# Other layouts for the moving operands and outputs of the products in a one-core encoder layer

## The chip, the cores and the metric

The kernel runs on one core of one Trainium2 chip. The metric is the time of the whole program on the device in microseconds, taken from the host's runs; a profiled execution gives the trace. Engines: PE (TensorE) multiplies, with its weight loads recorded apart as PEld; ACT (ScalarE), DVE (VectorE) and POOL (GpSimd) work on whole tiles; SP issues most DMAs. SBUF is the buffer that operands lie in, PSUM the accumulators that PE writes.

## What is computed

One layer of a streaming encoder on 320 token columns (256 of a prompt, 64 of a running stream), model width 2048. Cut to what the change touches:

```python
proj = xn @ w_in[l]                       # q, k, v, u, vs and two gates, 2048 columns each gate
a = stick_breaking(q, k, v)               # 8 heads x 128
bb = spatial_gate(u, vs, w_s, b_s)        # 8 groups x 128
gates = sigmoid(g + b_gate[l])
merged = g_a * (a @ w_branch_a[l]) + g_b * (bb @ w_branch_b[l])
h = x + merged @ w_out[l]
hn = rmsnorm(h, norm_ffn[l])
gu = hn @ w_gate_up[l]                    # D_FF = 5632
h = h + (silu(gu[..., :D_FF]) * gu[..., D_FF:]) @ w_down[l]
```

## The kernel before

Activations lie with features on the 128 partitions and the 320 token columns along them. Each float32 product is made from three products in the type float32r: weights and activations are each split into a rounded half (hi) and a rest (lo), and `product` adds hi times hi, hi times lo and lo times hi into one PSUM tile. One call of `product` is three matmuls of 128x128 weights with 320 moving columns: line 79 moves x[0] (hi) under the hi weights, line 80 moves x[1] (lo) under the same weights, line 81 moves x[0] under the lo weights.

`block` makes one output block of 128 features. It runs over its input blocks in groups of at most 8 (`HALF`): `weights` loads a group from HBM through SP (line 68), ACT makes its hi half (line 71), DVE its lo half (line 72), and then come the calls of `product`. Three PSUM tiles "acc" and four pairs of weight halves rotate.

`split` makes hi (ACT, line 113) and lo (DVE, line 114) of an activation, in two separate tiles "B" of 320 words a partition. Three families of activations go through it: the 8 heads' outputs `aT`, the 8 groups' outputs `bT`, and the hidden activations `act` of the feed-forward part. `gained` (lines 119 and 120) does the same for the inputs "A" with a gain per feature, and the merge makes its own pairs (mh, ml).

In order of time: the projections of q, k, v with attention woven in; v and u of the spatial gate; the merge, 16 times (two gate blocks from `w_in`, one block from `w_a` with `aT`, one from `w_b` with `bT`); 16 blocks of `w_out`; then three slices of the feed-forward part (16, 16 and 12 of its 44 blocks), each with its gate and up blocks from `w_gu` and 16 blocks of `w_down` that add to h. The last norm and the output follow.

A scheduler puts each engine's instructions in order by its own estimate; SP's order in the first stage is written by hand, and `tick`/`at` hang small pieces (attention, norms) between the groups of weights.

Of the kernel before, what the change touches and what calls it, by code (L numbers as in the profile page):

```python
# [9 lines left out]
F32R = mybir.dt.float32r  # L10
# [3 lines left out]
P = 128  # L14
TP = 256
TS = 64
T = TP + TS
D = 2048
KD = D // P
H = 8  # L20
# [3 lines left out]
SLICES = ((0, 16), (16, 16), (32, 12))  # L24
# [7 lines left out]
def stream_step(ctx: ExitStack, tc: tile.TileContext, xT, w_in, w_a, w_b, w_out, w_gu, w_down,  # L32
                gains, ws_t, bs, ck_t, cv, y_t, k_t, v_t, sv_t):
    nc = tc.nc
# [4 lines left out]
    big = pool("big")  # L39
# [3 lines left out]
    def acc():  # L43
        return psum.tile([P, 512], F32, tag="acc", bufs=3, name="acc")
# [15 lines left out]
    def tick():  # L60
        state["tick"] += 1
        for fn, a in later.pop(state["tick"], ()):
            fn(*a)


    def weights(src, n, view=lambda t: t):
        raw = wraw.tile([P, HALF * P], F32, tag="raw", name="raw")
        nc.sync.dma_start(out=view(raw[:, : n * P]), in_=src)
        wh = wsplit.tile([P, HALF * P], F32R, tag="wh", name="wh")
        wl = wsplit.tile([P, HALF * P], F32R, tag="wl", name="wl")  # L70
        nc.scalar.copy(out=wh[:, : n * P], in_=raw[:, : n * P])  # L71
        nc.vector.tensor_tensor(out=wl[:, : n * P], in0=raw[:, : n * P],  # L72
                                in1=wh[:, : n * P].bitcast(F32), op=ALU.subtract)
        return wh, wl

    def product(ps, w, j, x, first, last):
        wh, wl = w
        a, b = wh[:, j * P : (j + 1) * P], wl[:, j * P : (j + 1) * P]
        nc.tensor.matmul(ps[:, :T], a, x[0], start=first, stop=False)  # L79
        nc.tensor.matmul(ps[:, :T], a, x[1], start=False, stop=False)  # L80
        nc.tensor.matmul(ps[:, :T], b, x[0], start=False, stop=last)  # L81

    def block(src, act):

        ps = acc()
        nk = len(act)
        for k0 in range(0, nk, HALF):
            n = min(HALF, nk - k0)
            w = weights(src[:, k0 * P : (k0 + n) * P], n)
            for j in range(n):  # L90
                product(ps, w, j, act[k0 + j], k0 + j == 0, k0 + j == nk - 1)
            tick()
        return ps[:, :T]

    def slot(tag):
        return big.tile([P, T], F32R, tag=tag, bufs=32, name=tag)
# [11 lines left out]
            out.append(t[:, i % 2 * T : (i % 2 + 1) * T])  # L108
        return out, both

    def split(tag, src):
        hi, lo = slot(tag), slot(tag)
        nc.scalar.copy(out=hi, in_=src)
        nc.vector.tensor_tensor(out=lo, in0=src, in1=hi.bitcast(F32), op=ALU.subtract)
        return hi, lo
# [69 lines left out]
    xs = []  # L185
    first = [aux() for _ in range(3)]
# [12 lines left out]
    with tc.manual_schedule(engines={mybir.EngineType.SP}):  # L199
        load_x(*steps[0])  # L200
        for i, (c, n) in enumerate(steps):
            w = weights(w_qkv[0, :, :, c * P : (c + n) * P], 3 * n,
                        lambda t: t.rearrange("p (b k) -> p b k", b=3))
            if i + 1 < len(steps):
                load_x(*steps[i + 1])
            x = xp[c // 2]
            for m in range(c, c + n):
                xs.append(gained("A", x[:, m % 2 * T : (m % 2 + 1) * T], g_mix[:, m : m + 1]))
            for b in range(3):
                for j in range(n):  # L210
                    product(first[b], w, n * b + j, xs[c + j], c + j == 0, c + j == KD - 1)
            if c == 1:
                nc.scalar.activation(out=sqx, in_=x, func=AF.Square)
            elif c > 1:
                s = pair("xx")
                if c % 4:
                    nc.gpsimd.tensor_tensor(out=s, in0=x, in1=x, op=ALU.mult)
                else:
                    nc.scalar.activation(out=s, in_=x, func=AF.Square)
                (nc.gpsimd if c % 4 else nc.vector).tensor_tensor(out=sqx, in0=sqx, in1=s, op=ALU.add)  # L220
# [119 lines left out]
    def att_out(p, j):  # L340
        s = attn[p]
        (w0, w1), (vn, own_v), cvt = s["zm"], s["vn"][j], s["cv"]
        po = aux1()

        lo = 256 - 64 * j
        for i in range(3):
            v = cvt[:, i, j, :] if i < 2 else own_v
            nc.tensor.matmul(po[:, lo : lo + P], v, w1[:, 256 + i * P : 256 + (i + 1) * P],  # L348
                             start=i == 0, stop=i == 2)
        nc.tensor.matmul(po[:, 0:256], vn[:, 0, :], w0[:, j * 256 : (j + 1) * 256], start=True, stop=False)  # L350
        nc.tensor.matmul(po[:, 128:256], vn[:, 1, :], w1[:, j * P : (j + 1) * P], start=False, stop=True)
        aT[2 * p + j] = split("B", po[:, 0:T])

    aT: dict[int, tuple] = {}
    got = {}
# [35 lines left out]
    for g in range(H):  # L391
        ps = block(w_in[4 * H + g], xs)
        t = t320("ev")
# [18 lines left out]
    def sgu_mix(g):  # L412
        vn, own_v = vnat.pop(g)
        pg = aux()
        nc.tensor.matmul(pg[:, 256:384], own_v, wst[:, g, :], start=True, stop=True)
        nc.tensor.matmul(pg[:, 0:128], vn[:, 0, :], wst[:, g, :], start=True, stop=True)
        nc.tensor.matmul(pg[:, 128:256], vn[:, 1, :], wst[:, g, :], start=True, stop=True)
        b = t320("bb")
        for lo, n in ((0, 128), (128, 128), (256, 64)):
            nc.vector.tensor_tensor(out=b[:, lo : lo + n], in0=pg[:, lo : lo + n], in1=bsb[:, g, 0:n], op=ALU.add)  # L420
        nc.vector.tensor_tensor(out=b, in0=b, in1=us[g], op=ALU.mult)
        bT[g] = split("B", b)

    base = state["tick"]
    at(base + 1, sgu_norm)
# [3 lines left out]
    for g in range(H):  # L429
        ps = block(w_in[3 * H + g], xs)  # L430
        t = t320("ev")
# [6 lines left out]
    for m in range(KD):  # L438
        gate = []
        for i in range(2):  # L440
            ps = block(w_in[5 * H + i * KD + m], xs)
            t = t320("ev")
            nc.vector.tensor_tensor(out=t, in0=ps, in1=got["rx"], op=ALU.mult)
            gt = t320(f"gate{i}", 1)
            nc.scalar.activation(out=gt, in_=t, func=AF.Sigmoid, bias=b_gate[:, i * KD + m : i * KD + m + 1])
            gate.append(gt)
        if m == 0:
            att_ctx.close()
            mpool = mctx.enter_context(tc.tile_pool(name="merged", bufs=1))
        ps = block(w_a[m], [aT[h] for h in range(H)])  # L450
        t = t320("mg", 1)
        nc.vector.tensor_tensor(out=t, in0=ps, in1=gate[0], op=ALU.mult)
        ps = block(w_b[m], [bT[g] for g in range(H)])
        nc.vector.tensor_tensor(out=gate[1], in0=ps, in1=gate[1], op=ALU.mult)
        nc.vector.tensor_tensor(out=t, in0=t, in1=gate[1], op=ALU.add)
        hi = mpool.tile([P, T], F32R, tag="C", bufs=32, name="mh")
        lo = mpool.tile([P, T], F32R, tag="C", bufs=32, name="ml")
        nc.scalar.copy(out=hi, in_=t)
        nc.vector.tensor_tensor(out=lo, in0=t, in1=hi.bitcast(F32), op=ALU.subtract)
        merged.append((hi, lo))  # L460
# [4 lines left out]
    for m in range(KD):  # L465
        x = t320("xr")
        nc.gpsimd.dma_start(out=x, in_=xT[:, m, :])
        ps = block(w_out[m], merged)
# [8 lines left out]
    last = const.tile([P, T], F32, name="last")  # L477
    for s0, n in SLICES:
        act = []
        pend = []  # L480

        def finish(pg, pu):
            t = t320("ev")
            nc.vector.tensor_tensor(out=t, in0=pg, in1=got["rh"], op=ALU.mult)  # L484
            nc.scalar.activation(out=t, in_=t, func=AF.Silu)
            u = t320("bb")
            nc.vector.tensor_tensor(out=u, in0=pu, in1=got["rh"], op=ALU.mult)  # L487
            nc.vector.tensor_tensor(out=u, in0=u, in1=t, op=ALU.mult)
            act.append(split("B", u))

        for j in range(s0, s0 + n):
            pg = block(w_gu[j], hg)
            pu = block(w_gu[KF + j], hg)
            finish(pg, pu)
        for m in range(KD):
            ps = block(w_down[m][:, s0 * P : (s0 + n) * P], act)
            nc.vector.tensor_tensor(out=hs[m], in0=ps, in1=hs[m], op=ALU.add)  # L497
            if s0 + n < KF:
                continue
            if m == 0:  # L500

                nc.scalar.activation(out=warm, in_=hs[m][:, 0:1], func=AF.Sqrt, bias=eps_t, scale=0.0)
            if m < KD - 1:
                sqf.add(hs[m], nc.vector)
            else:
                nc.scalar.activation(out=last, in_=hs[m], func=AF.Square)
            nc.vector.tensor_scalar(out=hs[m], in0=hs[m], scalar1=g_fin[:, m : m + 1], scalar2=None, op0=ALU.mult)
# [3 lines left out]
    ps = aux1()  # L511
# [74 lines left out]
```

## Time and profile before

| | |
|---|---|
| median of 2 runs | 1736.17 us (1735.94 to 1736.4) |
| the profiled execution's own time | 1735.88 us |
| its span, first to last instruction | 1734.2 us |
| mean granted clock of PE | 0.996 |
| DVE busy | 862.4 us (50%) |
| ACT busy | 675.4 us (39%) |
| POOL busy | 68.5 us (4%) |
| HBM traffic | 151 GB/s over the span |

PE's rows overlap: a matmul's row runs from its start to the modelled end of its results, and the next one starts before that. So the time that a matmul takes from the span is read from the distance between starts, not from the mean length of a row.

### The profile page before, as it was taken

To read this page: it belongs to the slowest core of one execution; us is meant where nothing else is said; L and a number is where in the kernel's file an instruction comes from. 1 tells how busy PE (TensorE), PEld (TensorE's weight loads), DVE (VectorE), ACT (ScalarE), POOL (GpSimd) and SP (SyncE) were. 2 spreads that over 40 slices of the span, in tenths; PEclk is the share of its full clock that TensorE was granted. 3 is DMA by queue.
4 is the path that set the end of the run, shared out by engine and by line. 5 is a ranking of instruction groups with operands and counts; after the bars stand their busy time and mean duration, and the time that the engine had idled before them with its cause. 6 is when DMAs were issued, how large, how long until landed. Compare 5 with 4: busy or idle time off the path is not lost.

```text
span 1734.2 us, 27558 instructions
## 1 busy us (share of the span) xinstructions
PE 1710.1 (99%) x11656; PEld 1705.8 (98%) x11656; DVE 862.4 (50%) x1082; ACT 675.4 (39%) x833; POOL 68.5 (4%) x100
## 2 busy tenths in 40 slices
PE   7999999999999999999999999999999999999997
PEld 7999999999999999999999999999999999999997
DVE  7644456544444445555444444444444444444455
ACT  5644574433333333444333332233333333333342
POOL 4000001000000000220000000000000000000000
PEclk9999999999999999999999999999999999999998
DMA  7444434444444444554444454444444454444453
GB/s 248 163 158 163 147 120 146 134 146 148 153 149 147 154 150 155 175 174 146 149 153 148 148 153 149 147 154 149 147 152 152 146 150 154 146 151 153 129 152 110
DMA packets 77437, 263.20 MB, mean 152 GB/s; under 512 B 8961, under 2 KB 12929, under 8 KB 77313
## 3 DMA queue, kind: packets, MB, share of 16 engines
q1 hardware_dynamic: 74448, 252.74, 45.0%
q0 software_dynamic: 2720, 8.65, 1.5%
q8 instruction: 91, 1.49, 0.3%
q14 instruction: 34, 0.27, 0.0%
q10 hardware_dynamic: 144, 0.05, 0.0%
HBM read 255.90 MB, written 5.51 MB: 151 GB/s over the span
## 4 chain that ended last, share of the span: by engine, by line
PE 97%; DVE 1%; ACT 1%; issue 0%; DMA 0%; SPq 0%; DVEq 0%
PE acc L81 31%; PE acc L80 31%; PE acc L79 31%; DMA raw<-w_in 0%; DVE h L525 0%; DVE wl L72 0%; PE aux L348 0%; PE aux L329 0%; PE aux L81 0%; PE aux L273 0%; PE aux L79 0%; DVE A L120 0%; PE aux L80 0%; PE aux L350 0%; ACT wh L71 0%
## 5 line engine op out<-in xcount | busy, mean ns | idle before, releaser
L71 ACT CAST wh<-raw 128x1024 fp32r<-128x1024 f32 (+3 forms) x483 | 497.6, 1031 | 992.8 <-PE acc L80 811.3
L72 DVE TENSOR_TENSOR wl<-raw,wh 128x1024 fp32r<-128x1024 f32 (+3 forms) x483 | 583.7, 1208 | 519.3 <-ACT wh L71 516.7
L79 PE MATMUL acc<-A,wh 128*128 128x320 f32 x2512 | 779.2, 310 | 0.0
L81 PE MATMUL acc<-A,wl 128*128 128x320 f32 x2512 | 776.3, 309 | 0.5 <-DVE wl L72 0.5
L80 PE MATMUL acc<-A,wh 128*128 128x320 f32 x2512 | 776.2, 309 | 0.0
L81 PEld LDWEIGHTS acc<-A,wl 128*128 128x128 f32 x2512 | 471.5, 188 | 0.7 <-DVE wl L72 0.7
L80 PEld LDWEIGHTS acc<-A,wh 128*128 128x128 f32 x2512 | 471.7, 188 | 0.2
L79 PEld LDWEIGHTS acc<-A,wh 128*128 128x128 f32 x2512 | 471.6, 188 | 0.2
L81 PE MATMUL acc<-B,wl 128*128 128x320 f32 x960 | 296.6, 309 | 0.0
L79 PE MATMUL acc<-B,wh 128*128 128x320 f32 x960 | 296.6, 309 | 0.0
L80 PE MATMUL acc<-B,wh 128*128 128x320 f32 x960 | 296.6, 309 | 0.0
L79 PEld LDWEIGHTS acc<-B,wh 128*128 128x128 f32 x960 | 180.2, 188 | 0.0
L80 PEld LDWEIGHTS acc<-B,wh 128*128 128x128 f32 x960 | 180.2, 188 | 0.0
L81 PEld LDWEIGHTS acc<-B,wl 128*128 128x128 f32 x960 | 180.2, 188 | 0.0
L79 PE MATMUL acc<-mh,wh 128*128 128x320 f32 x256 | 79.1, 309 | 0.0
L80 PE MATMUL acc<-ml,wh 128*128 128x320 f32 x256 | 79.1, 309 | 0.0
L81 PE MATMUL acc<-mh,wl 128*128 128x320 f32 x256 | 79.1, 309 | 0.0
L487 DVE TENSOR_TENSOR bb<-acc,rh 128x320 f32<-128x320 f32 x44 | 21.6, 492 | 57.5 <-PE acc L81 57.5
L484 DVE TENSOR_TENSOR ev<-acc,rh 128x320 f32<-128x320 f32 x44 | 21.6, 492 | 56.6 <-PE acc L81 56.6
L497 DVE TENSOR_TENSOR h<-acc,h 128x320 f32<-128x320 f32 x48 | 23.5, 489 | 49.7 <-PE acc L81 49.7
L79 PEld LDWEIGHTS acc<-mh,wh 128*128 128x128 f32 x256 | 48.1, 188 | 0.0
L80 PEld LDWEIGHTS acc<-ml,wh 128*128 128x128 f32 x256 | 48.1, 188 | 0.0
(198 smaller groups left out, 744.6 us busy)
## 6 DMA issues: line engine op xcount, KB each, us to landing
raw<-w_gu SPq DMA_DIRECT2D x176, 512.0 KB, 3.5
raw<-w_in SPq DMA_DIRECT2D x138, 512.0 KB, 3.6
raw<-w_down SPq DMA_DIRECT2D x80, 512.0 KB, 3.5
raw<-w_out SPq DMA_DIRECT2D x32, 512.0 KB, 3.6
raw<-w_a SPq DMA_DIRECT2D x16, 512.0 KB, 3.5
raw<-w_b SPq DMA_DIRECT2D x16, 512.0 KB, 3.5
raw<-w_down SPq DMA_DIRECT2D x16, 256.0 KB, 2.7
raw<-w_in SPq DMA_DIRECT2D x7, 384.0 KB, 6.3
```

The lines of the kernel that those rows point to most:

```text
L71: nc.scalar.copy(out=wh[:, : n * P], in_=raw[:, : n * P])
L72: nc.vector.tensor_tensor(out=wl[:, : n * P], in0=raw[:, : n * P], in1=wh[:, : n * P].bitcast(F32), op=ALU.subtract)
L79: nc.tensor.matmul(ps[:, :T], a, x[0], start=first, stop=False)
L80: nc.tensor.matmul(ps[:, :T], a, x[1], start=False, stop=False)
L81: nc.tensor.matmul(ps[:, :T], b, x[0], start=False, stop=last)
L484: nc.vector.tensor_tensor(out=t, in0=pg, in1=got["rh"], op=ALU.mult)
L487: nc.vector.tensor_tensor(out=u, in0=pu, in1=got["rh"], op=ALU.mult)
L497: nc.vector.tensor_tensor(out=hs[m], in0=ps, in1=hs[m], op=ALU.add)
```

## The change

Five edits, none of which changes a value that is computed, or the number of matmuls.

1. `split` puts hi and lo in one tile "B2" of 640 words a partition in place of two tiles, 16 such tiles in place of 32 of half the size. How they lie in it is chosen by `layout`: 0 (the feed-forward part) has hi in words 0 to 319 and lo in 320 to 639; 1 (`aT`) has them word by word, hi in the even words and lo in the odd ones; 2 (`bT`) has them by runs of 160: hi, lo, hi, lo. So the moving operand of the `w_a` products goes in steps of two words, and that of the `w_b` products is two runs of 160 words, 160 words apart.
2. The gate blocks accumulate in columns 192 to 511 of their PSUM tile, not 0 to 319.
3. The gate blocks of the first feed-forward slice (j from 0 to 15) go by passes: within a group of 8 input blocks, all eight hi times hi, then all eight hi times lo, then all eight lo times hi.
4. `product` takes the PSUM columns from its caller, which changes nothing of the instruction.
5. `block` returns the columns that it wrote.

```diff
     def product(ps, w, j, x, first, last):
...
+        nc.tensor.matmul(ps, a, x[0], start=first, stop=False)
+        nc.tensor.matmul(ps, a, x[1], start=False, stop=False)
+        nc.tensor.matmul(ps, b, x[0], start=False, stop=last)
+
+    def passes(ps, w, n, act, k0, nk):
+
+        for i, (half, part) in enumerate(((0, 0), (0, 1), (1, 0))):
+            for j in range(n):
+                nc.tensor.matmul(ps, w[half][:, j * P : (j + 1) * P], act[k0 + j][part],
+                                 start=i == 0 and k0 + j == 0, stop=i == 2 and k0 + j == nk - 1)
+
+    def block(src, act, at_col=0, by_pass=False):
+
+        ps = acc()[:, at_col : at_col + T]
...
+            if by_pass:
+                passes(ps, w, n, act, k0, nk)
+            else:
+                for j in range(n):
+                    product(ps, w, j, act[k0 + j], k0 + j == 0, k0 + j == nk - 1)
...
-    def split(tag, src):
-        hi, lo = slot(tag), slot(tag)
+    def split(tag, src, layout=0):
+        t = big.tile([P, 2 * T], F32R, tag="B2", bufs=16, name="B")
+        if layout == 0:
+            hi, lo = t[:, 0:T], t[:, T : 2 * T]
+        elif layout == 1:
+            v = t[:, 0 : 2 * T].rearrange("p (t i) -> p i t", i=2)
+            hi, lo = v[:, 0, :], v[:, 1, :]
+        else:
+            v = t.rearrange("p (h i t) -> p i h t", i=2, h=2)
+            hi, lo = v[:, 0], v[:, 1]
+            src = src.rearrange("p (h t) -> p h t", h=2)
         nc.scalar.copy(out=hi, in_=src)
         nc.vector.tensor_tensor(out=lo, in0=src, in1=hi.bitcast(F32), op=ALU.subtract)
...
-        aT[2 * p + j] = split("B", po[:, 0:T])
+        aT[2 * p + j] = split("B", po[:, 0:T], 1)
...
-        bT[g] = split("B", b)
+        bT[g] = split("B", b, 2)
...
-            ps = block(w_in[5 * H + i * KD + m], xs)
+            ps = block(w_in[5 * H + i * KD + m], xs, 512 - T)
...
-            pg = block(w_gu[j], hg)
+            pg = block(w_gu[j], hg, by_pass=j < SLICES[1][0])
```

On PE, ACT, POOL and SP the instructions come in the same order as before, apart from the blocks by passes; on PE the strided `w_a` products stand where they stood and their rows read alike, since only the step within the operand differs. Three places show what can be seen of it. In the rows a number behind a name is the tile's own.

The first is PE at the start of the feed-forward part, where `sq_h` and `ones` are the operands of the norm's sum and mh, ml those of the last `w_out` block. Before:

```order
L81 MATMUL acc_7699<-mh_6621,wl_7733 128x320
L79 MATMUL acc_7771<-A_6698,wh_7774 128x320
L80 MATMUL acc_7771<-A_6699,wh_7774 128x320
L81 MATMUL acc_7771<-A_6698,wl_7775 128x320
L79 MATMUL acc_7771<-A_6767,wh_7774 128x320
L80 MATMUL acc_7771<-A_6768,wh_7774 128x320
L81 MATMUL acc_7771<-A_6767,wl_7775 128x320
```

After, with tile numbers left out, so that equal rows are counted:

```order
L81 MATMUL acc<-mh,wl 128x320
L87 MATMUL acc<-A,wh 128x320 x16
L87 MATMUL acc<-A,wl 128x320 x8
L178 MATMUL aux_7786<-sq_h,ones 128x320
L87 MATMUL acc<-A,wh 128x320 x16
L87 MATMUL acc<-A,wl 128x320 x8
L79 MATMUL acc<-A,wh 128x320
```

The lo weights (wl) are first read as the 17th matmul of a group, where it was the third, and the inputs of later blocks (A) are read earlier in it.

The second is DVE at the same place. Before:

```order
L120 SCALAR_TENSOR_TENSOR A<-h,gain,A 128x320
L161 TENSOR_SCALAR ev<-aux_7802 128x320
L72 TENSOR_TENSOR wl<-raw,wh 128x1024
L150 RECIPROCAL rh<-rh 128x320
L72 TENSOR_TENSOR wl<-raw,wh 128x1024
L151 SCALAR_TENSOR_TENSOR bb<-ev,rh 128x320
```

After:

```order
L139 SCALAR_TENSOR_TENSOR A<-h,gain,A 128x320
L72 TENSOR_TENSOR wl<-raw,wh 128x1024
L180 TENSOR_SCALAR ev<-aux_7786 128x320
L169 RECIPROCAL rh<-rh 128x320
L72 TENSOR_TENSOR wl<-raw,wh 128x1024
L170 SCALAR_TENSOR_TENSOR bb<-ev,rh 128x320
```

One weight split has moved ahead of the first step of the norm's factor `rh`; it is the only instruction that changes its place on DVE.

The third is ACT where the last groups' outputs `bT` are split, in the first pass of the merge. Before:

```order
L331 COPY vn<-aux 128x256
L333 COPY own_sgu_428<-aux 64x128
L113 CAST B<-bb 128x320
L71 CAST wh<-raw 128x1024 x2
L445 ACT_TABLE_LOAD
```

After:

```order
L350 COPY vn<-aux 128x256
L352 COPY own_sgu_428<-aux 64x128
L132 CAST B<-bb 128x2x160
L71 CAST wh<-raw 128x1024 x2
L464 ACT_TABLE_LOAD
```

Nothing has moved; the cast writes two runs of 160 words in place of one of 320.

More of the change, by code (lines that the diff above doesn't have):

```diff
@@ L78, in product @@
         a, b = wh[:, j * P : (j + 1) * P], wl[:, j * P : (j + 1) * P]
[L79 to L85, printed above, removed]
+        nc.tensor.matmul(ps, a, x[0], start=first, stop=False)
[8 more added lines that the diff above has]
+        ps = acc()[:, at_col : at_col + T]
         nk = len(act)
@@ L89, in block @@
             w = weights(src[:, k0 * P : (k0 + n) * P], n)
-            for j in range(n):
-                product(ps, w, j, act[k0 + j], k0 + j == 0, k0 + j == nk - 1)
+            if by_pass:
[3 more added lines that the diff above has]
+                    product(ps, w, j, act[k0 + j], k0 + j == 0, k0 + j == nk - 1)
             tick()
-        return ps[:, :T]
+        return ps
     def slot(tag):
@@ L210, in stream_step @@
                 for j in range(n):
-                    product(first[b], w, n * b + j, xs[c + j], c + j == 0, c + j == KD - 1)
+                    product(first[b][:, :T], w, n * b + j, xs[c + j], c + j == 0, c + j == KD - 1)
             if c == 1:
```

## The prediction

> **What bounds the kernel now.** I read the page's engine shares and chain first, then the waits of PE, then the merge stage by itself.
>
> ```profile
> span 1734.2 us, 27558 instructions
> PE 1710.1 (99%) x11656; PEld 1705.8 (98%) x11656; DVE 862.4 (50%) x1082; ACT 675.4 (39%) x833; POOL 68.5 (4%) x100
> ...
> PEclk9999999999999999999999999999999999999998
> ...
> PE 97%; DVE 1%; ACT 1%; issue 0%; DMA 0%; SPq 0%; DVEq 0%
> ```
>
> PE is busy for 99% of the span and makes 97% of the chain that ended last, at full granted clock. In the list of its waits the blocks "acc", which are all the work after the first stage but attention and norms, have one row (us in total, times, longest):
>
> ```profile
> PE acc L81 <- DVE wl L72: 0.5, 1, 0.5
> ```
>
> So this kernel's time is the number of matmuls times the distance between their starts, and a change of layout can matter only if it changes that distance. The merge stage gives the distance (us from:to, length, then busy us and count of PE and PEld):
>
> ```profile
> 345.08:676.10 331.02, 331.02 (x2260) 331.02 (x2259) 160.02 (x192) 121.83 (x143) 0.00 (x0) 1.00 0.45 150
> ```
>
> 331.02 / 2260 = 0.1465 us a matmul, or 0.458 ns for each of 320 moving columns. In this stage lie the products that get new layouts; L80 and L81 have a row like this one each:
>
> ```profile
> L79 PE MATMUL acc<-B,wh 128*128 128x320 f32 x256 | 79.1, 309 | 0.0
> ```
>
> 3 x 256 = 768 matmuls, half of them `w_a` (16 blocks x 8 heads x 3 = 384), half `w_b`.
>
> **What sets the distance.** Means by shape, of plain float32 matmuls (zm, sq_h), each of which is two passes in the trace, and of float32r ones (sph) with 512 and 128 columns:
>
> ```profile
> L350 PE MATMUL aux<-zm,vn 128*128 128x256 f32 x16 | 4.8, 380 | 0.0
> ...
> L351 PE MATMUL aux<-zm,vn 128*128 128x128 f32 x16 | 3.1, 274 | 0.0
> ...
> L305 PE MATMUL aux<-sph,negtr 128*128 128x512 f32 x4 | 1.6, 398 | 0.0
> ...
> L310 PE MATMUL aux<-sph,neg1r 128*128 128x128 f32 x4 | 0.9, 220 | 0.0
> ...
> L159 PE MATMUL aux<-sq_h,ones 128*128 128x320 f32 x2 | 0.7, 432 | 0.0
> ```
>
> Float32r grows by (398 - 220) / 384 = 0.464 ns a column. A plain pass grows by (380 - 274) / 128 = 0.83 ns. If a plain pass takes two steps of the array for each column, a step is 0.41 ns, and the float32r stream, at one step a column, runs about 11% slower than the array would allow. The starts of one group of sph (time, length) tell whether that surcharge belongs to the matmul or to the column:
>
> ```profile
> 82.85 0.40 PE L305 MATMUL aux<-sph,negtr 128*128 128x512 f32 x1
> 83.09 0.28 PE L306 MATMUL aux<-sph,neg1r 128*128 128x256 f32 x1
> 83.20 0.28 PE L307 MATMUL aux<-sph,negtr 128*128 128x256 f32 x1
> 83.32 0.34 PE L308 MATMUL aux<-sph,negtr 128*128 128x384 f32 x1
> 83.50 0.28 PE L309 MATMUL aux<-sph,neg1r 128*128 128x256 f32 x1
> 83.62 0.22 PE L310 MATMUL aux<-sph,neg1r 128*128 128x128 f32 x1
> 83.68 0.45 PE L305 MATMUL aux<-spl,negtr 128*128 128x512 f32 x1
> ```
>
> 1792 columns in 0.83 us are 0.463 ns a column whatever the length, so it is paid by the word moved. It appears where words are asked for at the full rate and not where they are asked for at half of it. I read it as the fetch of the moving words from SBUF being the limit already. That reading is the weak point of what follows.
>
> [...]
>
> **The change, part by part.**
>
> *Halves word by word (`w_a`).* 384 matmuls read every second word. The same number of matmuls is issued, so this is a price for each, and no row of the trace has a moving operand with a step. Lower end: 0, the 146.5 ns of the contiguous operand. Upper end: the dearest product of 320 columns that the trace holds, the plain float32 one, two passes (the x2 of its row) of 320 x 0.83 = 266 ns, 531 ns in all, which is 385 ns more, times 384 = +148 us. Between them: a fetch that brings in neighbouring words together, be it two or four, finds only half of them useful, so a stream limited by the fetch halves its rate, to 293 ns. That is +146.5 ns x 384 = +56.3 us. I take this value, since the surcharge above says that the stream has nothing to spare, and keep both ends.
>
> [...]
>
> *Halves by runs (`w_b`).* 384 matmuls have one jump of address in 320 words. Each new matmul of the timeline above begins at a new address too, and the one of 128 columns takes 83.68 - 83.62 = 0.06 us, the same 0.46 ns a column as the longer ones. So a jump costs nothing that the trace shows: 0, at most 1 ns x 384 = 0.4 us, the resolution of such a distance.
>
> *Columns 192 to 511 (gates).* L308 and L309 write from column 128 of their PSUM tile and L306 even in two runs, at the same 0.46 ns a column. 0 for these 32 blocks, and nothing in the read of them by DVE.
>
> *By passes (768 matmuls).* L79 and L80 share their weights, L80 and L81 share neither operand, L81 and the next L79 neither:
>
> ```profile
> 352.20 0.31 PE L79 MATMUL acc<-B,wh 128*128 128x320 f32 x1
> 352.35 0.31 PE L80 MATMUL acc<-B,wh 128*128 128x320 f32 x1
> 352.50 0.31 PE L81 MATMUL acc<-B,wl 128*128 128x320 f32 x1
> 352.64 0.31 PE L79 MATMUL acc<-B,wh 128*128 128x320 f32 x1
> ```
>
> Starts are 0.14 to 0.15 us apart in each case, and the page counts a weight load for each of its 11656 matmuls, so neither equal weights nor changed ones show in the time: 0. The order moves two needs. The lo weights are needed 14 matmuls (2 us) later, which can only relax the wait for DVE. The last input of the group is needed earlier, and one weight split goes ahead of the factor rh. For these, and for the one tile in place of two, DVE's timeline has the cover:
>
> ```profile
> 786.30 1.23 DVE L72 TENSOR_TENSOR wl<-raw,wh 128x1024 fp32r<-128x1024 f32 x1 [1.21 <-ACT wh L71]
> 788.88 0.49 DVE L469 TENSOR_TENSOR h<-acc,xr 128x320 f32<-128x320 f32 x1 [1.36 <-PE acc L81]
> ...
> 790.96 1.18 DVE L120 SCALAR_TENSOR_TENSOR A<-h,gain,A 128x320 fp32r<-128x320 f32 x1
> ...
> 799.58 0.49 DVE L153 SCALAR_TENSOR_TENSOR rh<-bb,rh 128x320 f32<-128x320 f32 x1
> ...
> 1634.22 0.49 DVE L487 TENSOR_TENSOR bb<-acc,rh 128x320 f32<-128x320 f32 x1 [1.31 <-PE acc L81]
> ...
> 1636.39 0.49 DVE L114 TENSOR_TENSOR B<-bb,B 128x320 fp32r<-128x320 f32 x1 [0.53 <-ACT B L113]
> ```
>
> The last `w_out` block ends just before 788.9, and the first feed-forward block begins there. Its last input's lo half is ready at 790.96 + 1.18 = 792.1; by passes it is read as matmul 24 + 16 of the block, 39 x 0.1465 = 5.7 us in, at about 794.6: 2.5 us of cover. The factor rh is ready at 800.1, later by at most one weight split of 1.23 us. It is needed to empty the first of three PSUM tiles before the fourth block starts, 3 x 48 x 0.1465 = 21.1 us after 788.9, at 810: some 8 us of cover. And where a `w_down` product might now wait for both halves of one tile: the last of them is ready at 1636.39 + 0.49 = 1636.9, while the slice of 12 needs it as the 34th matmul after about 1634.1, at 1638.9: 2 us of cover. If one of these failed, it would cost one to three microseconds, once or three times.
>
> *The writes of the halves.* The eight `aT` splits on DVE are these:
>
> ```profile
> L114 DVE TENSOR_TENSOR B<-aux,B x8: 483/484/492, 97.7 to 253.2; 128x320 fp32r<-128x320 f32 x8
> ```
>
> The last is done at 253.7 and the first `w_a` product reads it at 352.2, so even twice the 0.48 us is hidden by 98 us of other work. The `bT` splits write runs of the same length in all, at the same place.
>
> **Sum.** The profiled execution took 1735.9 us: its span of 1734.2 and 1.7 around it. 1735.9 + 56.3 + 0 + 0 + 0 = 1792.2 us. The median of the runs is 1736.2, so 1792.5 on its scale; I predict 1792.
>
> **The rivals.**
>
> *The fetch has slack, nothing changes (not slower).* If the 11% surcharge is a matter of the type float32r itself, for instance of a conversion on the way in, the fetch may be far from its limit, and every second word costs what every word costs: 1736 us, give or take 2. For it: the surcharge is the same 0.46 ns in all stages, whatever DVE and ACT do at the same time. It decides if the fetch can bring in, with every second word useful, the same 320 words in 146.5 ns, that is pass over twice the stretch of SBUF in that time. [...]
>
> *The surcharge grows, but the rate is not halved.* If only the 0.05 ns over the array's step doubles, a matmul takes 0.51 x 320 = 163 ns, +17 ns x 384 = +6 us: 1742. At any price under 1.62 times (34.7 us / 384 = 90 ns) the result stays within 2%. [...]
>
> *A word fetched alone costs as much as a plain float32 product.* The upper end above: 1736 + 148 = 1884 us. Against it: the instructions keep their type and their number.
>
> *Faster.* 2% are 34.7 us. The passes hold 768 x 0.1465 = 112.5 us, which would have to shrink by a third through their order, and the even starts of L79, L80 and L81 speak against any gain.
>
> **How the numbers follow.** Halved rate in `w_a`: 0.58. No change: 0.28. Partial: 0.07. Dearer than halved: 0.04. Faster: 0.03. A change of under 2% is about what a measurement of this kernel cannot tell from none. Slower by over 2% is the first and the fourth, 0.62; within 2% the second and the third, 0.35; faster 0.03. For the likeliest case alone 1785 to 1800 us (1.9 to 2.1 times the distance, and 2 us for the covers). Since the case of no change holds more than 0.2, the range has to reach it: 1734 to 1800 holds all but the dearest and the gain, which is more than 8 in 10, but a narrower one would hold less.
>
> **What would show it.** In the profile after, the starts of the `w_a` matmuls in the merge stage tell step one: 0.29 us apart if the fetch halves, 0.15 if it has slack. The merge stage should then last 331 + 56 us, and every other stage what it lasts now; the gate blocks, the `w_b` blocks and the blocks by passes should keep 0.1465 us a matmul. PE's waits in "acc" should stay under 2 us. The prediction is wrong if `w_a` keeps its pace, or if any of the other three layouts loses it.

## The result and the profile after

| | us |
|---|---|
| before, median | 1736.17 (1735.94 to 1736.4, 2 runs) |
| changed, median | 1791.04 (1790.67 to 1791.4, 2 runs) |
| ratio | 1.0313, 95% interval [1.0296, 1.0329] |
| span of the profiled execution | 1789.7 (before: 1734.2) |

The change costs 3.1%. The lines of the changed kernel's page that answer to those of before:

```profile
span 1789.7 us, 27558 instructions
PE 1767.8 (99%) x11656; PEld 1731.7 (97%) x11656; DVE 861.1 (48%) x1082; ACT 677.6 (38%) x833; POOL 68.9 (4%) x100
...
PEclk9999999999999999999999999999999999999998
...
PE 97%; ACT 1%; DVE 1%; DMA 1%; SPq 0%; issue 0%; DVEq 0%; ACTq 0%
```

The same number of instructions, a mean granted clock of 0.994 (0.996 before), PE still busy for 99%: it only takes longer for the same matmuls. The stretches of the merge and of the `w_out` blocks (from:to, length, then busy us and count of PE, PEld, DVE, ACT and POOL):

```profile
345.64:731.37 385.73, 385.73 (x2258) 354.68 (x2257) 160.07 (x192) 121.81 (x143) 0.00 (x0) 1.00 0.41 128
731.37:844.00 112.63, 112.63 (x770) 112.63 (x769) 63.67 (x65) 46.42 (x63) 22.97 (x28) 1.00 0.55 170
```

The merge takes 385.7 us where it took 331.0; 54.7 of the 55.5 us by which the span grew lie there. PE's timeline at the start and the end of the first `w_a` block (start, length):

```profile
352.61 0.31 PE L81 MATMUL acc<-A,wl 128*128 128x320 f32 x1
352.76 0.44 PE L79 MATMUL acc<-B,wh 128*128 128x320 f32 x1
353.02 0.46 PE L80 MATMUL acc<-B,wh 128*128 128x320 f32 x1
353.31 0.48 PE L81 MATMUL acc<-B,wl 128*128 128x320 f32 x1
353.60 0.48 PE L79 MATMUL acc<-B,wh 128*128 128x320 f32 x1
...
359.70 0.33 PE L79 MATMUL acc<-B,wh 128*128 128x320 f32 x1
359.87 0.31 PE L80 MATMUL acc<-B,wh 128*128 128x320 f32 x1
360.02 0.31 PE L81 MATMUL acc<-B,wl 128*128 128x320 f32 x1
360.16 0.31 PE L79 MATMUL acc<-B,wh 128*128 128x320 f32 x1
```

From the first `w_a` matmul at 352.76 to the first `w_b` matmul at 359.70 are 24 distances, 6.94 / 24 = 0.289 us each. The `w_b` ones, read by runs, are back at 0.147. A matmul's row also grows, from 0.31 to 0.48 us, and no row of these shows a wait for another engine.

### The profile page after: what moved, and what is told of

The parts are those of the page before. It is cut to its first block, busy times and chain, and to the rows that moved or that the text cites. A ratio compares the mean times of both kernels' runs of the same rounds, so it can differ in the third digit from the quotient of the medians.

```text
span 1789.7 us, 27558 instructions
## 1 busy us (share of the span) xinstructions
PE 1767.8 (99%) x11656; PEld 1731.7 (97%) x11656; DVE 861.1 (48%) x1082; ACT 677.6 (38%) x833; POOL 68.9 (4%) x100
## 4 chain that ended last, share of the span: by engine, by line
PE 97%; ACT 1%; DVE 1%; DMA 1%; SPq 0%; issue 0%; DVEq 0%; ACTq 0%
PE acc L80 29%; PE acc L79 29%; PE acc L81 29%; PE acc L87 6%; DMA raw<-w_in 1%; DVE wl L72 0%; DVE h L544 0%; PE aux L367 0%; PE aux L81 0%; PE aux L348 0%; PE aux L292 0%; ACT wh L71 0%; PE aux L79 0%; PE aux L80 0%; PE aux L369 0%; PE aux L288 0%
## 5 line engine op out<-in xcount | busy, mean ns | idle before, releaser
L79 PE MATMUL acc<-A,wh 128*128 128x320 f32 x2256 | 699.9, 310 | 0.0
L81 PE MATMUL acc<-A,wl 128*128 128x320 f32 x2256 | 697.1, 309 | 0.5 <-DVE wl L72 0.5
L80 PE MATMUL acc<-A,wh 128*128 128x320 f32 x2256 | 697.0, 309 | 0.0
L81 PEld LDWEIGHTS acc<-A,wl 128*128 128x128 f32 x2256 | 423.5, 188 | 0.7 <-DVE wl L72 0.7
L80 PEld LDWEIGHTS acc<-A,wh 128*128 128x128 f32 x2256 | 423.6, 188 | 0.2
L79 PEld LDWEIGHTS acc<-A,wh 128*128 128x128 f32 x2256 | 423.6, 188 | 0.2
L79 PE MATMUL acc<-B,wh 128*128 128x320 f32 x960 | 317.5, 331 | 0.0
L80 PE MATMUL acc<-B,wh 128*128 128x320 f32 x960 | 317.4, 331 | 0.0
L81 PE MATMUL acc<-B,wl 128*128 128x320 f32 x960 | 317.2, 330 | 0.0
L80 PEld LDWEIGHTS acc<-B,wh 128*128 128x128 f32 x960 | 182.9, 191 | 10.3
L79 PEld LDWEIGHTS acc<-B,wh 128*128 128x128 f32 x960 | 182.9, 191 | 10.3
L87 PE MATMUL acc<-A,wh 128*128 128x320 f32 x512 | 80.5, 309 | 0.0
L87 PEld LDWEIGHTS acc<-A,wh 128*128 128x128 f32 x512 | 76.5, 188 | 0.2
```

Source lines behind the costliest of these rows:

```text
L79: nc.tensor.matmul(ps, a, x[0], start=first, stop=False)
L80: nc.tensor.matmul(ps, a, x[1], start=False, stop=False)
L81: nc.tensor.matmul(ps, b, x[0], start=False, stop=last)
L87: nc.tensor.matmul(ps, w[half][:, j * P : (j + 1) * P], act[k0 + j][part], start=i == 0 and k0 + j == 0, stop=i == 2 and k0 + j == nk - 1)
```

## The experiments

Each comes with its edit, what was expected of it before it ran, and what was measured. Distances between starts are means over the 24 matmuls of one block, worked out from the starts in that run's trace, in ns.

### One part undone: aT next to each other

```diff
-        aT[2 * p + j] = split("B", po[:, 0:T], 1)
+        aT[2 * p + j] = split("B", po[:, 0:T])
```

> The changed kernel with one part undone: the aT halves lie next to each other (320 words of hi, then 320 of lo), all else stays changed (runs in w_b, gate columns 192 to 511, passes, one tile for both halves). Theory (the whole price is the fetch of every second word in the 384 w_a matmuls): 1736.2 us plus 384 x 1 ns for the runs, so 1736 to 1737, ratio to before 1.000. Rival (part of the price is in the runs, the columns, the passes or the shared tiles): above 1738; up to 1791 if the step were innocent.

Measured: 1736.31 us, ratio 0.9998 [0.9989, 1.0008]. The runs, the columns, the passes and the shared tiles together cost nothing that can be measured.

### One part alone: word by word in the kernel before

```diff
-    def split(tag, src):
-        hi, lo = slot(tag), slot(tag)
+    def split(tag, src, words=False):
+        t = big.tile([P, 2 * T], F32R, tag="B2", bufs=16, name="B")
+        if words:
+            v = t.rearrange("p (t i) -> p i t", i=2)
+            hi, lo = v[:, 0, :], v[:, 1, :]
+        else:
+            hi, lo = t[:, 0:T], t[:, T : 2 * T]
...
-        aT[2 * p + j] = split("B", po[:, 0:T])
+        aT[2 * p + j] = split("B", po[:, 0:T], True)
```

> The kernel before with one part added: halves in one tile, word by word for aT and next to each other for bT and act; gate columns, passes and runs as before. Theory (fetch of every second word): 1736.2 + 384 x (289 - 146.5) ns = 1790.9 us, 1790 to 1792, and 0.289 us between starts in w_a. Rival (the parts act together): anything clearly under 1790.

Measured: 1789.86 us, ratio 1.0307 [1.0289, 1.0324]. The whole loss comes with this part. The time is a little under the forecast, since only the first w_a block ran at 289 ns and the other fifteen at 284; 15 x 24 x 5 ns are 1.8 us.

### The cost doubled: bT word by word too

```diff
-        bT[g] = split("B", b, 2)
+        bT[g] = split("B", b, 1)
```

> The changed kernel with the suspected cost doubled: bT lies word by word too, so that w_a and w_b, 768 matmuls, read every second word. Theory (each such matmul pays 289 - 146.5 ns, nothing else): 1736.2 + 768 x 142.5 ns = 1845.6 us, 1844 to 1848. Rival (part of the 55 us is a price paid once, as by the late waits of the merge): clearly under 1840.

Measured: 1842.85 us, ratio 1.0613 [1.0595, 1.0631]. Twice as many stepped matmuls cost 106 us, nearly twice the 55: a price for each matmul, 106 us / 768 = 138 ns. The forecast of 1844 to 1848 was a little high, since most blocks here ran at 283 to 285 ns and not at 289 to 290, as with this part alone. Blocks of one layout differ by these 5 ns; the cause is open.

### Sixteen orders of reading

```diff
+    def read(t, at, *dims):
+        a = t[:, 0:1]
+        return bass.AP(a.tensor, a.offset + at, [list(a.ap[0])] + [list(d) for d in dims])
...
-        ps = block(w_a[m], [aT[h] for h in range(H)])
+        ps = block(w_a[m], [tuple(read(t, *p) for p in PATTERNS[m]) for t in aW])
```

> The aT halves lie next to each other, and each of the 16 w_a blocks reads 320 words of those tiles in another order, so the values of the w_a products are not the reference's. Blocks m = 0 to 15: 0 and 15 in order; 1 every second word; 2 pairs of words with a pair left out between; 3 the same beginning at word 1; 4 runs of four words with four left out; 5 the same beginning at word 2; 6 the same beginning at word 1; 7 runs of eight with eight left out; 8 every third word; 9 every fourth; 10 every eighth; 11 every word twice; 12 every word four times; 13 one word 320 times; 14 in order from word 1. ns between starts. Theory L (fetch by lines of four words, 1.81 ns a line, floor 0.42 ns a column): 0, 4, 7, 14, 15: 146; 1, 2, 3, 5, 6: 289; 8: 433; 9, 10: 578; 11, 12, 13: about 136. Theory P (fetch by aligned pairs, 0.90 ns a pair): 0, 2, 4, 5, 7, 14, 15: 146; 6: 217; 1, 3, 8, 9, 10: 289; 11, 12, 13: about 136. Theory S (a step over 1 in the innermost dimension halves the rate, whatever it touches): 1, 8, 9, 10: 289, all others 146. Rival on the surcharge (the 0.46 ns belong to the type float32r, not to the fetch): 11, 12, 13 stay at 146. Whole time, L: 1736 + 24 x (5 x 142 + 287 + 2 x 432 - 3 x 10) ns = 1780 us; P: 1736 + 24 x (71 + 5 x 142 - 30) ns = 1754 us; S: 1750 us.

| block | words read | measured | L | P | S |
|---|---|---|---|---|---|
| 0, 15 | in order | 146.7 | 146 | 146 | 146 |
| 1 | every second | 289 | 289 | 289 | 289 |
| 2 | pairs, a pair left out | 289 | 289 | 146 | 146 |
| 3 | the same from word 1 | 289 | 289 | 289 | 146 |
| 4 | runs of four | 146.5 | 146 | 146 | 146 |
| 5 | the same from word 2 | 289 | 289 | 146 | 146 |
| 6 | the same from word 1 | 285 | 289 | 217 | 146 |
| 7 | runs of eight | 147 | 146 | 146 | 146 |
| 8 | every third | 283 | 433 | 289 | 289 |
| 9 | every fourth | 289 | 578 | 289 | 289 |
| 10 | every eighth | 271 | 578 | 289 | 289 |
| 11, 12 | every word twice, four times | 135.8 | 136 | 136 | 146 |
| 13 | one word 320 times | 135.8 | 136 | 136 | 146 |
| 14 | in order from word 1 | 151 | 146 | 146 | 146 |

All three theories fall: P and S on the pairs (2) and on the runs of four that begin within a line (5, 6), L on the wide steps (8 to 10). Two things stand. Lines of four words (16 bytes), counted from the tile's first word, matter here, since the same runs of four cost 146.5, 289 or 285 ns by whether they begin at word 0, 2 or 1 of one. And the surcharge goes with the order of the words and not with the type: in the same type it is gone where words are read again (135.8 ns, in order 146.7). PE's timeline at block 12, every word four times:

```profile
633.12 0.30 PE L79 MATMUL acc<-B,wh 128*128 128x320 f32 x1
633.26 0.30 PE L80 MATMUL acc<-B,wh 128*128 128x320 f32 x1
633.39 0.30 PE L81 MATMUL acc<-B,wl 128*128 128x320 f32 x1
633.53 0.30 PE L79 MATMUL acc<-B,wh 128*128 128x320 f32 x1
```

0.41 us for three are 0.136 each, where words in order take 0.147. The whole run took 1763.12 us (one run), between what L and P gave.

### Plain float32

```diff
+        if plain:
+            a, b, x = a.bitcast(F32), b.bitcast(F32), [v.bitcast(F32) for v in x]
...
-        aT[2 * p + j] = split("B", po[:, 0:T], 1)
+        aT[2 * p + j] = split("B", po[:, 0:T], 1 if p < 2 else 0)
...
-        ps = block(w_a[m], [aT[h] for h in range(H)])
+        ps = block(w_a[m], [aT[h] for h in range(H)], plain=True)
```

> The changed kernel with the w_a products in plain float32 (two passes a matmul, each asking for words at half the rate), aT word by word for heads 0 to 3 and next to each other for heads 4 to 7. Theory (the fetch has a rate of its own, 289 ns for 320 stepped words, and is seen only where the array is faster): contiguous passes 268 ns apart, stepped ones 289; whole time 1736 + 192 x 2 x (268 + 289) - 384 x 146.5 ns = 1736 + 158 = 1894 us. Rival (each stepped matmul pays 142 ns more whatever its rate): stepped passes 410 ns apart, 1940 us. Rival (a stepped pass halves its rate): 536 ns, 1988 us.

Measured: 1891.38 us (one run). In PE's timeline a row is now a product of two passes; the first three below read every second word, the last three read in order:

```profile
358.30 0.72 PE L81 MATMUL acc<-B,wh 128*128 128x320 f32 x2
358.86 0.72 PE L82 MATMUL acc<-B,wh 128*128 128x320 f32 x2
359.42 0.72 PE L83 MATMUL acc<-B,wl 128*128 128x320 f32 x2
...
361.60 0.70 PE L81 MATMUL acc<-B,wh 128*128 128x320 f32 x2
362.13 0.70 PE L82 MATMUL acc<-B,wh 128*128 128x320 f32 x2
362.67 0.70 PE L83 MATMUL acc<-B,wl 128*128 128x320 f32 x2
```

0.56 us for two passes are 280 ns a pass with the step; without it the starts give 269. So the step does not double what a matmul takes, and the rivals' 410 and 536 ns are excluded. It adds 11 ns to a pass of plain float32, where it adds 142 to a float32r matmul. That fits the theory, by which the step is seen only where a matmul is otherwise faster, though its 289 ns for a stepped pass were a little high; its reason, a fetch with a rate of its own, is not shown by these rows.

### Runs of four

```diff
-            v = t.rearrange("p (h i t) -> p i h t", i=2, h=2)
+            v = t.rearrange("p (h i t) -> p i h t", i=2, h=2 if layout == 2 else T // 4)
...
-        aT[2 * p + j] = split("B", po[:, 0:T], 1)
+        aT[2 * p + j] = split("B", po[:, 0:T], 4)
```

> The changed kernel with aT in runs of four words: four of hi, four of lo, and so on; the same step between tiles, the same jumps, 80 of them in a matmul. Theory (full rate wherever four words in a row lie in one line of four): 1736 to 1737 us, 0.146 us between starts in w_a. Rival (interleaving as such, or the number of jumps, is what costs): over 1750, up to 1791.

Measured: 1736.33 us, ratio 0.9997 [0.9987, 1.0006], 146.4 ns in w_a. Here interleaved halves cost nothing where four words of one half lie in a line.

### More orders, and bfloat16

The edit is that of the first study with other patterns; in blocks 10 to 15 both operands are bfloat16 copies made from float32 words of aT, the same copies in every matmul.

> As the first study of orders, the values of the w_a products are not the reference's: each w_a block reads 320 elements of the aT tiles in another order. Blocks 0 to 9 in float32r: 0 in order; 1 runs of ten, next run 12 on; 2 one word twice, next word 4 on; 3 one word twice, next word 2 on; 4 the four words of each line backwards; 5 the four words of a line in the order 0, 2, 1, 3; 6 every second word; 7 runs of 16 from word 2, next run 32 on; 8 in order from word 4; 9 in order from word 2. Blocks 10 to 15 with operands and weights in bfloat16 (eight to a line): 10 in order; 11 every second; 12 every fourth; 13 every eighth; 14 pairs with a pair left out; 15 runs of four with four left out. ns between starts. Theory G (0.458 ns an element where at least four in a row lie in one line, never under 136 ns; 0.90 ns for each other element): 0, 4, 5, 8, 9: 146; 3: 136 to 146; 2, 6: 289; 1: 174; 7: 182; 10, 11, 14, 15: 136; 12, 13: 289. Rival B (the whole line must be read in ascending order): 3, 4, 5: 289, and 11, 14, 15: 289 too. [...] Rival for bfloat16 (half the bytes, so stepped reads have twice the slack): 12 and 13 under 200.

| block | elements read | measured | G |
|---|---|---|---|
| 0, 8, 9 | in order from word 0, 4, 2 | 146.7, 145.6, 146.5 | 146 |
| 1 | runs of ten | 173 | 174 |
| 2 | a word twice, next word 4 on | 289 | 289 |
| 3 | a word twice, next word 2 on | 146.7 | 136 to 146 |
| 4, 5 | each line backwards; 0, 2, 1, 3 | 146.7 | 146 |
| 6 | every second | 289 | 289 |
| 7 | runs of 16 from word 2 | 180 | 182 |
| 10 | bfloat16, in order | 136 | 136 |
| 11, 14, 15 | bfloat16, every second; pairs; runs of four | 142 | 136 |
| 12 | bfloat16, every fourth | 283 | 289 |
| 13 | bfloat16, every eighth | 563 | 289 |

Rival B falls on blocks 3 to 5 (146.7 ns) and the rival for bfloat16 on blocks 12 and 13 (283 and 563). G fits all of float32r, but bfloat16 in steps of eight takes 563 ns, twice what it allows. PE's timeline there:

```profile
638.65 0.72 PE L87 MATMUL acc<-half 128*128 128x320 bf16 x1
639.19 0.74 PE L88 MATMUL acc<-half 128*128 128x320 bf16 x1
639.76 0.74 PE L89 MATMUL acc<-half 128*128 128x320 bf16 x1
640.32 0.74 PE L87 MATMUL acc<-half 128*128 128x320 bf16 x1
```

Per change of a line of 16 bytes, bfloat16 gives 142 / 80, 283 / 160 and 563 / 320, each time 1.76 to 1.78 ns: the count of theory L, which float32r had refuted. Both would agree if in float32r the changes of line are counted apart for the elements at even and at odd places of the order, at about 1.8 ns each (an estimate: 289 ns / 160 for every second word). Every fourth word then has 160 changes in each half and not 320 in one count; it took 289 ns. That is theory U of the next run, which puts it as two streams. The run took 1758.95 us (one run).

### Two streams or four in a row

The edit is again that of the first study.

> A third study of orders (float32r; the values of the w_a products are not the reference's), to tell two readings of the first two apart. Theory G: at least four elements in a row must lie in one line of four words, else 0.90 ns an element. Theory U: the elements with even and with odd number within the operand are fetched by two separate streams, each of which takes about 1.8 ns for every change of line, and the array takes 136 ns for 320 columns at best. Blocks 0 to 15, words in the order read: 0 in order; 1 t and 320 + t in turn (0, 320, 1, 321, ...); 2 t and 160 + t in turn; 3 as 1, from word 1; 4 2t and 320 + 2t in turn; 5 4t and 4t + 3 in turn; 6 t, 80 + t, 160 + t, 240 + t in turn; 7 eight such areas of 40 in turn; 8 t and t + 2 in turn; 9 t and t + 6 in turn; 10 runs of eight in order (as 0); 11 within each eight words 0, 4, 1, 5, 2, 6, 3, 7; 12 pairs of words t of a line with pairs of words 320 on in turn; 13 every second word, each twice; 14 every second word; 15 in order. ns between starts by U: 0, 10, 13, 15: 146; 1, 2, 3, 8, 9, 11: 136; 4, 12: 146; 5, 6, 7, 14: 289. By G: 0, 10, 13, 15: 147; 8: about 182; 1 to 7, 9, 11, 12, 14: 289.

| block | words read | measured | U | G |
|---|---|---|---|---|
| 1, 2 | t and 320 + t; t and 160 + t, in turn | 135.8 | 136 | 289 |
| 3 | as 1, from word 1 | 136.5 | 136 | 289 |
| 4, 12 | 2t and 320 + 2t; pairs of two areas | 146.7 | 146 | 289 |
| 5 | 4t and 4t + 3 | 289 | 289 | 289 |
| 6 | four areas of 80 in turn | 170 | 289 | 289 |
| 7 | eight areas of 40 in turn | 272 | 289 | 289 |
| 8 | t and t + 2 | 136.3 | 136 | 182 |
| 9, 11 | t and t + 6; 0, 4, 1, 5, 2, 6, 3, 7 | 135.8 | 136 | 289 |
| 0, 10, 13, 15 | in order; each second word twice | 146.7 | 146 | 147 |
| 14 | every second | 289 | 289 | 289 |

PE's timeline at block 1:

```profile
374.18 0.30 PE L79 MATMUL acc<-B,wh 128*128 128x320 f32 x1
374.32 0.30 PE L80 MATMUL acc<-B,wh 128*128 128x320 f32 x1
374.45 0.30 PE L81 MATMUL acc<-B,wl 128*128 128x320 f32 x1
374.59 0.30 PE L79 MATMUL acc<-B,wh 128*128 128x320 f32 x1
```

Reading two areas in turn (135.8 ns) is faster here than reading one in order (146.7). G falls on nine blocks. U fails on block 6 (170 for 289), and on block 7 it is 6% too high (272 for 289), as it is on every eighth word of the first study (271 for 289). In blocks 6 and 7 the elements at even places go back and forth between two areas or four; no run shows why that costs less than U's count. The run took 1744.88 us (one run).

### Word by word, read in turns

```diff
-            v = t[:, 0 : 2 * T].rearrange("p (t i) -> p i t", i=2)
-            hi, lo = v[:, 0, :], v[:, 1, :]
+            v = t.rearrange("p (h t i) -> p i t h", i=2, h=2)
+            hi, lo = v[:, 0], v[:, 1]
+            src = src.rearrange("p (t h) -> p t h", h=2)
```

> The changed kernel with its word by word layout of aT kept (hi in the even words, lo in the odd ones), but with the even token columns in the first 320 words and the odd ones in the last 320, read in turns: words 0, 320, 2, 322 and so on. Every matmul of w_a still uses two of the four words of each line that it touches and still touches 160 lines. Theory U (two streams, each pays about 1.8 ns for every change of line): each stream finds two of its words in a row in a line, 80 changes, so 146.7 ns as block 4 of the third study, and 1736 to 1737 us. Rival (half-used lines as such are what costs, 160 lines at 1.8 ns): 289 ns, 1790 to 1792 us.

Measured: 1736.47 us, ratio 0.9999 [0.9989, 1.0009]. PE's timeline at the start of w_a:

```profile
353.21 0.31 PE L79 MATMUL acc<-B,wh 128*128 128x320 f32 x1
353.35 0.31 PE L80 MATMUL acc<-B,wh 128*128 128x320 f32 x1
353.50 0.31 PE L81 MATMUL acc<-B,wl 128*128 128x320 f32 x1
353.65 0.31 PE L79 MATMUL acc<-B,wh 128*128 128x320 f32 x1
```

The starts are 0.147 us apart. Half of each line is still left out, and the price is gone. So it is not the half-used line that costs. Theory U, by which the changes of line within each half of the order are counted, 80 here and 160 with the step of two, gave the measured time.

### A kernel faster than both: every operand read in turns

```diff
+    def turns(t):
+        return t.rearrange("p (i t) -> p t i", i=2)
+
     def split(tag, src):
-        hi, lo = slot(tag), slot(tag)
+        hi, lo = turns(slot(tag)), turns(slot(tag))
+        src = src.rearrange("p (t i) -> p t i", i=2)
```

and the same in `gained` and for mh and ml, in the kernel before.

> The kernel before, with the 320 words of every hi and lo half (A, B, mh, ml) stored with the even token columns first (words 0 to 159) and the odd ones behind (160 to 319), and every product reading them in turns, word t and word 160 + t, so that the outputs stand in PSUM as before. Theory U: each of the two streams reads its words in order, four to a line, half as many lines as now: 136 ns a matmul in place of 146.6, 11328 matmuls less 11 ns = 122 us less, 1610 to 1625 us, if DMA, ACT and DVE keep up with 3.3 us for each group of weights. Theory G: never four in a row in one line, 289 ns, over 3300 us. Rival (the surcharge is not lost although the lines are halved, as a jump at every word has a price of its own): 1736 us or more.

Measured: 1622.35 us (1619.97 to 1623.08), ratio 0.9339 [0.9323, 0.9354]: 6.6% faster than the kernel before. From its page:

```profile
span 1620.7 us, 27558 instructions
PE 1591.1 (98%) x11656; PEld 1585.8 (98%) x11656; DVE 888.4 (55%) x1082; ACT 706.0 (44%) x833; POOL 66.0 (4%) x100
...
PE 93%; DVE 2%; ACT 2%; issue 1%; DMA 1%; SPq 0%; DVEq 0%; ACTq 0%
```

The trace gives 136 ns between starts in all stages, and the work from the first "acc" matmul on is 118.1 us shorter than before. Against it stands the first stage: its first "acc" matmul comes at 41.4 us, before at 36.8. PE's wait there for DVE's halves of the weights has grown from 4.7 us to this:

```profile
PE aux L81 <- DVE wl L72: 8.6, 4, 4.4
```

In that stage ACT and DVE also make the halves of x, whose words now jump between two areas:

```profile
L124 ACT ACTIVATE A<-x,gain x16: 807/856/910, 3.5 to 33.0; 128x320 fp32r<-128x320 f32 x16
L125 DVE SCALAR_TENSOR_TENSOR A<-x,gain,A x16: 766/792/3499, 4.4 to 36.9; 128x320 fp32r<-128x320 f32 x16
```

Their medians before were 560 and 552 ns. That these longer rows cause the later start is the likely reading; no run separates it. The splits "B" of the later stages have grown too:

```profile
L117 ACT CAST B<-bb 128x320 fp32r<-128x320 f32 x52 | 41.4, 797 | 13.6 <-DVE bb L426 8.2 <-DVE bb L494 1.3
L118 DVE TENSOR_TENSOR B<-bb,B 128x320 fp32r<-128x320 f32 x52 | 37.9, 730 | 6.7 <-ACT B L117 6.7
```

They took 460 and 486 ns before. A gain of 118.1 less 4.65 is the 113.5 us by which the span fell.

### Weights word by word

```diff
-        wh = wsplit.tile([P, HALF * P], F32R, tag="wh", name="wh")
-        wl = wsplit.tile([P, HALF * P], F32R, tag="wl", name="wl")
+        both = wsplit.tile([P, 2 * HALF * P], F32R, tag="wb", name="wb")
+        both = both.rearrange("p (k i) -> p i k", i=2)
+        wh, wl = both[:, 0, :], both[:, 1, :]
```

> The kernel before with hi and lo of the weights word by word in one tile, for all products; activations as before. All weight loads read every second word, 128 of them. Theory (a rate of 0.90 ns a word holds for this port too, and the load lies beside the matmul before it): 128 x 0.90 = 115 ns are hidden under 146.5 ns, and ACT and DVE write stepped words at no price, so 1736 to 1738 us. Rival (the loads share the fetch with the moving words, or a stepped load does not fit beside a matmul): 0.16 us or more between starts, over 1890 us.

Measured: 1737.17 us, ratio 1.0006 [0.9996, 1.0015]. The matmuls' starts keep their mean of 147 ns, and a weight load's row is 197 ns where it was 188; before and in this run:

```profile
L80 PEld LDWEIGHTS acc<-A,wh 128*128 128x128 f32 x2512 | 471.7, 188 | 0.2
```

```profile
L80 PEld LDWEIGHTS acc<-A,wb 128*128 128x128 f32 x2512 | 494.3, 197 | 0.3
```

Stepped weights cost this kernel nothing. The 115 ns that the theory put for a load are not shown by these rows. One thing was not as expected: ACT's casts to the stepped hi halves took 1105 ns on average, before 1031, which did not lengthen the run; DVE's halves kept their time, 1210 against 1208.

## Why the prediction was right

- **The forecast.** 1792 us was put and 1791.04 measured. The range from 1734 on would have held no change as well, so it is the starts 0.289 us apart and the length of the merge that bear out the halved rate.
- **The bound.** That the time is the number of matmuls times their distance held: the page after shows the same shares, and 54.7 of 55.5 us lie in the one stage where the distance changed.
- **Word by word, +56.3 us.** Measured 54.7 in the stage, with 289 ns a matmul where 293 was taken. The case without this part (ratio 0.9998) and the case with it alone (1.0307) show that it is the whole of it.
- **Why it halves.** Two sentences carried the price, and both were the author's estimate of what lies behind the distances. The first was that the surcharge is the fetch's. The runs show that it goes with the order in which words are read: 146.7 ns in order, 135.8 with words read again and 135.8 with two areas read in turns. Its size is 146.7 over 135.8, 8% and not 11%. The step of 0.41 ns was half of a plain pass, and that a plain pass takes two steps was assumed; measured are 269 ns for a plain pass and 135.8 for the shortest float32r matmul, 0.42 ns a column. The second, that a fetch brings neighbours together and half of them are useless, gave the right size by a rule that the runs refute, and so partly by luck. A fetch of two words would have left pairs cheap, and one of four would have made every fourth word four times as dear; pairs cost 289 and every fourth word 289, and the half-used lines of the word by word layout in turns cost nothing (1736.47 us against 1736.6). What fits is a count, an estimate from these distances: about 1.8 ns (289 / 160) for each change of line, counted apart for the words at even and at odd places, and never under 135.8 ns. That is 160 changes for every second word, 80 in order, 40 in turns. Of the float32r orders tried one does not follow it (170 for 289), two lie 6% below it, and the others within 4%. How the words get to PE no run shows.
- **The rival of no change.** It took the surcharge for the type's own, and words read again in the same type lose it (135.8 ns). It needed 320 words in 146.5 ns with every second word useful, and they took 289. Nor is it the number of words used of a line that decides: the layout read in turns uses two of four, as every second word does, and takes 146.7.
- **The partial rival.** 163 ns were too low: the 289 measured are 1.97 times the 146.7.
- **The dearest case.** It needed 531 ns a matmul and is excluded by the 289.
- **Runs, columns, passes.** 0 us, as put; the distances after are 147, 147 and 147 ns.
- **The covers.** They held. PE's only wait in "acc" is again one of 0.5 us:

```profile
PE acc L81 <- DVE wl L72: 0.5, 1, 0.5
```

The writes word by word cost DVE nothing (485 ns at the median, before 484), where twice was allowed for. They cost ACT a little, 460 ns at the median where the same eight casts took 425 before, which the prediction had not looked at and the same cover hid:

```profile
L132 ACT CAST B<-aux x8: 435/460/463, 97.5 to 253.4; 128x320 fp32r<-128x320 f32 x8
L133 DVE TENSOR_TENSOR B<-aux,B x8: 483/485/493, 98.3 to 253.8; 128x320 fp32r<-128x320 f32 x8
```

## What to carry to other kernels

Where matmuls stand back to back, look at the distance of their starts per moving column and compare types and orders: in order float32r took 0.46 ns a column (146.7 / 320) and bfloat16 0.42 (136 / 320), and in float32r the distance followed the layout of the moving operand, from 135.8 to 289 ns. The PSUM columns, the order of passes and the layout of the weights did not change the time of this kernel. If float32r words that PE moves have to be interleaved, runs of four that begin on a line of four words cost nothing here (146.4 ns), while word by word, read with a step of two, doubled the distance (289 ns). Storing even columns ahead of odd ones and reading the two areas in turns took this kernel from 1736.9 to 1622.4 us; it is worth a trial wherever float32r matmuls fill the time and ACT and DVE can bear slower writes (here 797 and 730 ns a split, before 460 and 486).

## What had not been expected of the hardware

Reading a float32r operand in order was not the fastest way: 146.7 ns for 320 columns, against 135.8 when the operand alternates between two areas. bfloat16 fits a single count of changes of line: 136 ns in order and 142, 283 and 563 ns with four, two and one elements used of each 16 bytes. In the splits of aT a step of two words in what is written costs DVE nothing (485 ns against 484), and ACT 35 ns (460 against 425); 797 ns on ACT and 730 on DVE is what the splits take when the words jump between areas 160 words apart, and DVE then reads the hi half in that order too.
